# Two gate projections as seven products of quarters at the head of a layer, and the first products of two MLP groups side by side, in a two-layer hybrid encoder

## The chip, the cores and the metric

The kernel runs on one core of a Trainium2 chip. The metric is device time in microseconds of one execution of the whole program, which is both layers. Three runs of the kernel before gave 2899.88, 2901.86 and 2904.1 us; the median is 2901.86 us.

## What is computed

640 tokens (512 of one prompt, and 8 groups of 16) of width 1024 go through two layers in fp32. A layer is an RMS norm, one wide projection that feeds three mixers, a merge by gates, an output projection, and an MLP:

```
u = rms_norm(x, norm1_g);  z = u @ w_in
(xa, ga, mq, mk, mv, mo, mi, mf, aq, ak, av, g_a, g_b, g_c) = split(z)
y_a = (rg_lru(conv(xa)) * gelu(ga)) @ w_oa            # branch a
y_b = (rms_norm(mlstm(mq, mk, mv, ...)) * sigmoid(mo)) @ w_ob   # branch b
y_c = banded_sink_attention(rope(aq), rope(ak), av) @ w_oc      # branch c
mix = sigmoid(g_a + b0) * y_a + sigmoid(g_b + b1) * y_b + sigmoid(g_c + b2) * y_c
x = x + mix @ w_out
x = x + square(relu(rms_norm(x, norm2_g) @ w_up)) @ w_down
```

The three gate projections g_a, g_b and g_c are 1024 by 1024 each. The scale of the norm depends on the token alone, so the kernel multiplies it in after a projection.

## The kernel before

Every fp32 product is made of three products of a rounded high part and a low rest (hi·hi, hi·lo, lo·hi). A weight job loads 1 MB from DRAM into `wraw`, and each quarter of it is split by ScalarE (line 164, `whi`) and VectorE (line 166, `wlo`). `jobs` is the list of the weight jobs in the order in which the program takes them (lines 325 to 351); `next_w` prepares one job ahead.

`gemm_w` makes 256 output channels: two accumulators `acc` (there are two such buffers) of 48 matmuls of 320 columns each, 96 per job. A gate of one branch is four such jobs. `strassen_w` makes 256 channels of `w_up` with seven products of half-sized blocks in place of eight, 84 matmuls of 320 columns; VectorE adds the blocks of weights (`wsum`) and ScalarE and VectorE split the sums too. In before it serves the MLP alone.

A layer of before runs in this order: norm; the recurrent branch (LRU), whose projections run in turn with its scans; two jobs of gate b; attention (`attention`, with a third and a fourth job of gate b, and `branch_a(0)`, in it); `branch_a(1)` to `branch_a(3)`, each of which is a job of gate a and a job of `w_oa`; the mLSTM, head after head; four jobs of gate c, `gate(2)`; the merge; the output projection; the MLP. What the text writes is not what the engines run: a scheduler sorts the instructions by simulated times and priorities, and each engine then runs its own list in order. A job that comes later in the text is so drawn forward into places where an earlier stage waits, as far as its operands and its buffers allow.

Attention takes the heads in eight pairs (`prompt_pair`). For a pair, TensorE makes the scores (L847), VectorE takes the maxima (L822, L823), ScalarE the exponentials (L825, L826), VectorE the quotient (L827 to L830), TensorE transposes (L869), ScalarE and VectorE copy the result out (L871), and TensorE multiplies by the values (L877). Two groups of decode tokens (`sample_group`, L901 to L937) follow the fourth and the eighth pair. In the mLSTM a head's prompt chunks pass a state from one to the next (L672 to L690), and its decode tokens load, update and store eight state blocks (`sample`: L577 the keys' round trip over DRAM, L585 the load of a block `cb`, L589 and L590 its split, L593 and L597 the products, L599 the update, L601 the store).

The norm (`norm_scale`, L378 to L394) sums squares by matmuls with `ones` (L383), computes `rtok` in a chain of small VectorE instructions (L120 to L125), and spreads it over the partitions (L392 to L394) as `rbc`. Every evacuation of a projection multiplies by `rbc`.

Of the kernel before, what the change touches and what calls it, by code (L numbers as in the profile page):

```python
# [75 lines left out]
def trunk(ctx: ExitStack, tc: tile.TileContext, I, O):  # L76
# [92 lines left out]
    def prep(j, *hfs):  # L169
        ap, n, kind = jobs[j]  # L170
        out = ready.setdefault(j, [])
        if kind == "d":
# [6 lines left out]
            return  # L179
        if kind == "s":  # L180
# [9 lines left out]
            out.append(parts(a11, 128))  # L190
            s1 = add(a21, a22, ALU.add)
            yield
            out.append(parts(s1, 128))
# [12 lines left out]
            out.append(parts(s3, 128))  # L206
            out.append(last)
            yield
            return
# [22 lines left out]
    def next_w():  # L232
        j = cur[0]
        cur[0] += 1
        finish(j)
        if jobs[j][2] == "w":
            finish(j + 1)
        else:
            step()
        return ready.pop(j)  # L240

    def strassen_w(xs, epi):

        w = next_w()
# [4 lines left out]
        def product(nm):  # L249
            ws = w[("p1", "p5", "p2", "p3", "p6", "p7", "p4").index(nm)]  # L250
            first = nm in ("p1", "p5", "p2")
# [65 lines left out]
    for l in range(depth):  # L317
        win = I["w_in"][l]

        def cols(c, n=256):  # L320
            return (win[:, c:c + n], n)
# [4 lines left out]
        gc = [cols(C_G[2] + 256 * j) for j in range(4)]  # L326
        oa, ob, oc, ow = [[(I[nm][l][:, 256 * j:256 * j + 256], 256) for j in range(4)] for nm in ("w_oa", "w_ob", "w_oc", "w_out")]
        for k, j in LRU_ORDER:
            jobs.append(cols((C_XA, C_GA)[k] + 256 * j))
        jobs += [gb[0], gb[1], cols(C_AKV), gb[2]]  # L330
        for j in range(4):
            if j == 3:
                jobs += [ga[0], oa[0]]
            jobs.append(cols(C_AQ - 8, 264) if j == 0 else cols(C_AQ + 256 * j))
            if j == 1:
                jobs.append(gb[3])
        for j in range(1, 4):
            jobs += [ga[j], oa[j]]
        for j in range(4):
            jobs += seq[j]  # L340
        jobs += gc + oc + ob
        jobs += [ow[0], ow[2], ow[1], ow[3]]
        for kind, i in MLP_ORDER[l == depth - 1]:
            if kind == "s":
                jobs.append((I["w_up"][l][:, 256 * i:256 * i + 256], 256, "s"))
# [63 lines left out]
    cv, cvh = vectors(0)  # L409
    xpool = tc.tile_pool(name="xp0", bufs=8)  # L410
    xp = xpool.__enter__()
    with tc.tile_pool(name="ld", bufs=1) as ld:
# [19 lines left out]
        for m in range(8):  # L432
# [16 lines left out]
        dve.tensor_tensor(vv[:, 0:5], xss[:, 0:5], xss[:, 5:10], ALU.add)  # L449


# [287 lines left out]
    def attention(l, ap):  # L739
# [206 lines left out]
        for j in range(4):  # L946
# [11 lines left out]
            if j == 3:  # L958
                branch_a(0)
# [24 lines left out]
    for l in range(depth):  # L984
# [17 lines left out]
        norm_scale(vv[:, 0:5] if l == 0 else None)  # L1002
        xpool.__exit__(None, None, None)
        if l > 0:
            hdpool.__exit__(None, None, None)

        ngate = [0, 0, 0]
        kept = []

        def gate(i, keep=False):  # L1010
            def evac(m, acc):
# [4 lines left out]
                act.activation(sg, sg, AF.Tanh, bias=half(V_BG + i, k), scale=0.5)  # L1016
                if keep:
                    kept.append(sg)
                else:
                    act.dma_start(gdr[i][128 * k:128 * k + 128, :], sg)  # L1020
            gemm_w(u, evac)

        def branch_a(j):

            gate(0, True)

            def evac(m, acc):
                sg = kept.pop(0)
                dve.scalar_tensor_tensor(halves(sg), halves(sg), 1.0, acc[:, :, 0:320], op0=ALU.add, op1=ALU.mult)
                k = 2 * j + m  # L1030
                sp.dma_start(mdr[128 * k:128 * k + 128, :], sg)
            gemm_w(hg, evac)
# [174 lines left out]
        gate(1)  # L1207
        gate(1)
        with tc.tile_pool(name="at", bufs=1, reuse_waits="tile") as ap:
# [8 lines left out]
        gtp = gtpool.__enter__()  # L1218
        for j in range(1, 4):
            branch_a(j)  # L1220
            if j == 1:
                mlstm_gates(l, gp, gtp)
        hgpool.__exit__(None, None, None)
# [16 lines left out]
        xpool = tc.tile_pool(name=f"xp{l + 1}", bufs=8, reuse_waits="tile")  # L1240
        xp = xpool.__enter__() if l < depth - 1 else ctx.enter_context(xpool)
# [75 lines left out]
        dve.tensor_tensor(tt[:, 0:5], rtok[:, 0:5], rtok[:, 0:5], ALU.mult)  # L1317

# [12 lines left out]
        def up(i):  # L1331
# [36 lines left out]

            product = strassen_w(operand, epi)
            before = pend[0]  # L1370
# [19 lines left out]

        for n, (kind, i) in enumerate(MLP_ORDER[last]):
            if kind == "s":
# [72 lines left out]
```

## Time and profile before

| quantity | value |
|---|---|
| median of three runs | 2901.86 us |
| the profiled execution | 2899.9 us |
| its span in the trace | 2898.1 us |
| mean granted TensorE clock | 0.995 of full speed |
| TensorE matmul busy | 2839.4 us, 98% |
| VectorE busy | 1853.8 us, 64% |
| ScalarE busy | 1312.4 us, 45% |

PE is TensorE's matmul row, PEld its weight loads, DVE is VectorE, ACT is ScalarE, SP the engine that issues most DMAs. Matmuls overlap in their pipeline, so their busy time is longer than the time from one issue to the next. A granted clock of 1.00 is 2.4 GHz, and 0.5 is 1.2 GHz.

### The profile page before, as it was taken

Reading aid. Unit: us, or ns where it says so; the run is one execution under the profiler, and the core shown is the slowest. Engines: PE = TensorE matmul, PEld = TensorE weight load, DVE = VectorE, ACT = ScalarE, POOL = GpSimd, SP = SyncE. Lnnn points to the kernel's source line nnn. Section 1 sums busy time; section 2 is a strip of 40 time slices with the busy share of each in tenths; the row PEclk is TensorE's granted clock in tenths of the full one; section 3 lists DMA queues with packets and bytes.
Section 4 is the critical chain, followed back from the end, with each engine's and each line's share of the span. In section 5 each row is a group of like instructions: output and inputs, shape, how many; then the busy total and the mean of one; then the engine's idle time right before and its main releaser. Section 6 shows DMA issues by size and latency. Waiting matters only on the chain. (4 is left out here: it accounts for less than half of the span.)

```text
span 2898.1 us, 50789 instructions
## 1 busy us (share of the span) xinstructions
PE 2839.4 (98%) x20134; PEld 2799.9 (97%) x20134; DVE 1853.8 (64%) x3758; ACT 1312.4 (45%) x2767; POOL 26.7 (1%) x65
## 2 busy tenths in 40 slices
PE   8999999999999999999999999999999999999999
PEld 8999999999999999999999999999999999999999
DVE  7967566444565677676679676655445646667772
ACT  5764444333442445444357544443444324443452
POOL 0000000000000000000000000000000000000000
PEclk9999999999999999999999999999999999999999
DMA  5242224444573322222322322334445733222222
GB/s 174 65 123 81 76 82 123 120 136 138 158 259 125 104 72 81 81 80 81 113 67 79 116 73 84 96 101 147 131 141 152 264 110 102 74 88 73 80 81 81
DMA packets 276878, 319.53 MB, mean 110 GB/s; under 512 B 26424, under 2 KB 231016, under 8 KB 276608
## 3 DMA queue, kind: packets, MB, share of 16 engines
q1 hardware_dynamic: 267104, 300.03, 33.8%
q10 hardware_dynamic: 9536, 16.26, 1.6%
q8 instruction: 158, 2.59, 0.4%
q14 instruction: 80, 0.66, 0.1%
HBM read 255.76 MB, written 62.04 MB: 110 GB/s over the span
## 5 line engine op out<-in xcount | busy, mean ns | idle before, releaser
L293 PE MATMUL acc<-at,whi 128*128 128x320 f32 x5120 | 818.0, 312 | 6.9 <-ACT at L133 2.8
L293 PEld LDWEIGHTS acc<-at,whi 128*128 128x128 f32 x5120 | 765.3, 189 | 10.2 <-ACT at L133 3.4
L164 ACT CAST whi<-wraw 128x512 fp32r<-128x512 f32 x680 | 406.9, 619 | 512.7 <-PE acc L293 186.9
L166 DVE TENSOR_TENSOR wlo<-wraw,whi 128x512 fp32r<-128x512 f32 x680 | 451.3, 693 | 173.7 <-ACT whi L164 113.5
L311 PE MATMUL acc<-whi,at 128*128 128x256 f32 (+1 forms) x3040 | 408.5, 284 | 16.9 <-DVE qT L626 4.5
L293 PE MATMUL acc<-at,wlo 128*128 128x320 f32 x2560 | 415.6, 310 | 0.0
L311 PEld LDWEIGHTS acc<-whi,at 128*128 128x128 f32 x3040 | 378.2, 188 | 22.1 <-DVE qT L626 5.5
L293 PEld LDWEIGHTS acc<-at,wlo 128*128 128x128 f32 x2560 | 384.1, 188 | 0.7
L255 PE MATMUL acc<-at,whi 128*128 128x320 f32 x1536 | 266.9, 314 | 8.4 <-ACT at L130 5.5
L255 PEld LDWEIGHTS acc<-at,whi 128*128 128x128 f32 x1536 | 236.9, 191 | 14.4 <-ACT at L130 6.1
L311 PE MATMUL acc<-wlo,at 128*128 128x256 f32 (+1 forms) x1520 | 218.6, 282 | 0.2 <-DVE wlo L166 0.2
L311 PEld LDWEIGHTS acc<-wlo,at 128*128 128x128 f32 x1520 | 196.4, 188 | 0.6 <-DVE wlo L166 0.5
L277 PE MATMUL psb<-at,whi 128*128 128x320 f32 x896 | 171.1, 309 | 0.0
L277 PE MATMUL acc<-at,whi 128*128 128x320 f32 x896 | 169.0, 309 | 0.0
L255 PE MATMUL acc<-at,wlo 128*128 128x320 f32 x768 | 143.8, 310 | 0.0
L277 PEld LDWEIGHTS psb<-at,whi 128*128 128x128 f32 x896 | 141.6, 188 | 0.0
L277 PEld LDWEIGHTS acc<-at,whi 128*128 128x128 f32 x896 | 140.9, 188 | 0.0
L164 ACT CAST whi<-wsum 128x512 fp32r<-128x512 f32 x128 | 79.0, 619 | 129.1 <-PE acc L277 93.3
L255 PEld LDWEIGHTS acc<-at,wlo 128*128 128x128 f32 x768 | 121.5, 190 | 0.0
L166 DVE TENSOR_TENSOR wlo<-wsum,whi 128x512 fp32r<-128x512 f32 x128 | 87.8, 689 | 46.9 <-ACT whi L164 45.1
L277 PE MATMUL acc<-at,wlo 128*128 128x320 f32 x448 | 101.8, 308 | 0.0
L277 PE MATMUL psb<-at,wlo 128*128 128x320 f32 x448 | 100.6, 308 | 0.0
(372 smaller groups left out, 3613.1 us busy)
## 6 DMA issues: line engine op xcount, KB each, us to landing
wraw<-in_w_in SPq DMA_DIRECT2D x160, 512.0 KB
wraw<-in_w_up SPq DMA_DIRECT2D x64, 512.0 KB
wraw<-in_w_down SPq DMA_DIRECT2D x64, 512.0 KB
cb<-in_state_mlstm_C SPq DMA_DIRECT2D x64, 256.0 KB
out_C_s<-cb SPq DMA_DIRECT2D x64, 256.0 KB
gdr<-sg ACTq DMA_DIRECT2D x32, 320.0 KB
rl<-ydr SPq DMA_DIRECT2D x32, 320.0 KB
sg<-gdr SPq DMA_DIRECT2D x32, 320.0 KB
```

The source lines that it names most:

```text
L164: act.copy(hi if shape else hi[:, :, :src.shape[-1]], src)
L166: dve.tensor_tensor(lo if shape else lo[:, :, :src.shape[-1]], src, h.bitcast(F32), ALU.subtract)
L255: pe.matmul(bank[nm], ws[i][:, k, :], xs(nm, k)[:, part], start=(first and i == 0 and k == 0 and part == 0), stop=(i == 1 and k == 3), ski ...
L277: pe.matmul(o[s], lhs, hs[k][:, part, 320 * s:320 * s + 320], start=(k == 0 and i == 0 and part == 0), stop=(i == 1 and k == 3))
L293: pe.matmul(acc[:, s, 0:320], lhs, xs[k][:, part, 320 * s:320 * s + 320], start=(i == 0 and k == 0 and part == 0), stop=(i == 1 and k == 7),)
L311: pe.matmul(o, xs[k][:, part, 128 * t:128 * t + 128], wt[:, k % KQ, 0:n], start=(i == 0 and k == 0 and part == 0), stop=(i == 1 and k == 7),)
```

## The change

Gates a and c are computed first in a layer, right after two jobs of gate b, by `strassen_gates`: eight jobs through `strassen_w`, with 84 matmuls in place of 96. Before that, VectorE and ScalarE form the sums of the activations that the seven products need (`t12`, `t34`: four pairs of tiles). The gates are written to DRAM (`gdr`), and gate a is read back by `branch_a`, which is now a job of `w_oa` alone. `branch_a(1)` stands where `branch_a(0)` stood, `branch_a(0)` moves one step ahead; a job of gate b stands at the end of the LRU and one in attention. No gate is left between `branch_a` and the mLSTM's end, and after the mLSTM the attention's output is reloaded with no job between.

In the MLP, the groups 0 and 1 of `w_up` begin side by side: their first products are issued in turn, and `norm_scale` stands behind them. For that the first two operands of group 1 are loaded early and its raw weights are loaded a second time (job kinds `e` and `r`).

```diff
+    out += [("e", 1), ("s", 0), ("r", 1)]
     for i in range(15):
-        out.append(("s", i))
+        if i > 1:
+            out.append(("s", i))
...
+        jobs += [gb[0], gb[1]]
+        jobs += [(a, n, "s") for a, n in ga + gc]
         for k, j in LRU_ORDER:
             jobs.append(cols((C_XA, C_GA)[k] + 256 * j))
-        jobs += [gb[0], gb[1], cols(C_AKV), gb[2]]
+        jobs += [gb[2], cols(C_AKV), gb[3]]
         for j in range(4):
             if j == 3:
-                jobs += [ga[0], oa[0]]
+                jobs.append(oa[1])
             jobs.append(cols(C_AQ - 8, 264) if j == 0 else cols(C_AQ + 256 * j))
             if j == 1:
-                jobs.append(gb[3])
-        for j in range(1, 4):
-            jobs += [ga[j], oa[j]]
+                jobs.append(oa[0])
+        jobs += oa[2:]
         for j in range(4):
             jobs += seq[j]
-        jobs += gc + oc + ob
+        jobs += oc + ob
...
+    def strassen_gates(l, ut, u, xs, vec, half):
+        t12, t34, xg = [], [], {}
+        for i in range(4):
+            for k in (i, 4 + i):
+                xg[k] = ut.tile([128, NT], F32, name="xg", tag="xg", bufs=2)
+                act.activation(xg[k], xs[k], AF.Copy, scale=vec(V_N1, k))
+            a, b = xg[i], xg[4 + i]
+            t = ut.tile([128, NT], F32, name="ut12", tag="ut12", bufs=1)
+            dve.tensor_tensor(t[:, 0:320], a[:, 320:640], a[:, 0:320], ALU.subtract)
+            dve.tensor_tensor(t[:, 320:640], b[:, 320:640], t[:, 0:320], ALU.subtract)
+            t12.append(act_tile(ut))
+            split(t12[i], t)
...
+            return strassen_w(operand, epi)
...
+        with tc.tile_pool(name="ut", bufs=8, reuse_waits="tile") as ut:
+            sums[0] = ut
+            gate(1)
+            gate(1)
+            strassen_gates(l, ut, u, xs, vec, half)
...
         def branch_a(j):
-            gate(0, True)
-
             def evac(m, acc):
-                sg = kept.pop(0)
+                k = 2 * j + m
+                sg = tr.tile([128, NT], F32, name="sg", tag="sg")
+                with tc.issue_after(wlast[0].ins):
+                    sp.dma_start(sg, gdr[0][128 * k:128 * k + 128, :])
...
         gate(1)
-        gate(1)
         with tc.tile_pool(name="at", bufs=1, reuse_waits="tile") as ap:
             attention(l, ap)
...
-        for j, n in enumerate((4, 0, 3, 0)):
-            yc += reload(ydr[1], hdp, range(len(yc), len(yc) + n))
-            gate(2)
-        yc += reload(ydr[1], hdp, range(7, 8))
+        yc += reload(ydr[1], hdp)
...
-        norm_scale()
-
-        dve.tensor_tensor(rbc, rbc, rbc, ALU.mult)
...
+        early, early_run = {1: next_w()}, (0, 1)
+        p_0 = up(0)
+        p_0("p1")
+        p_0("p5")
+        p_1 = up(1)
+        p_1("p1")
+        p_1("p5")
...
+        norm_scale()
```

TensorE, the seventh pair of attention's eight, in the kernel before (L847 the scores, L869 the transposes, L293 matmuls of `gemm_w`):

```order
L847 MATMUL psb<-kh_2338,qp_2361 128x64 x2
L847 MATMUL psb<-kh_2338,qp_2361 128x128 x2
L847 MATMUL psb<-kh_2338,qp_2361 128x192 x12
L293 MATMUL acc<-at,whi 128x320 x23
L293 MATMUL acc<-at,wlo 128x320 x16
L293 MATMUL acc<-at,whi 128x320 x4
L869 MATMUL psb<-cs,prob_2368 128x128 x2
L293 MATMUL acc<-at,whi 128x320 x2
L869 MATMUL psb<-cs,prob_2369 128x128 x4
L293 MATMUL acc<-at,whi 128x320 x6
L869 MATMUL psb<-cs,prob_2370 128x128 x4
L869 MATMUL psb<-cs,prob_2371 128x128 x4
```

The same place in the changed kernel (L930 scores, L952 transposes, L960 products with the values, L1052 and L1054 the next queries' transposes):

```order
L930 MATMUL psb<-kh_3684,qp_3707 128x64 x2
L930 MATMUL psb<-kh_3684,qp_3707 128x128 x2
L930 MATMUL psb<-kh_3684,qp_3707 128x192 x12
L952 MATMUL psb<-cs,prob_3714 128x128 x2
L952 MATMUL psb<-cs,prob_3715 128x128 x4
L960 MATMUL psb<-pT,vd 128x256
L952 MATMUL psb<-cs,prob_3716 128x128 x4
L952 MATMUL psb<-cs,prob_3717 128x128 x4
L960 MATMUL psb<-pT,vd 128x256 x2
L1052 MATMUL psb<-cs,q 128x128 x4
L960 MATMUL psb<-pT,vd 128x256 x4
L1054 MATMUL psb<-cs,q 128x128
```

In this place 51 of `gemm_w`'s matmuls stand between the scores and the last transposes of before, and none in the changed kernel; the three other pairs of attention's second half read the same there, in both layers. The jobs that stood here are gates, which are now at the layer's head, and jobs of `w_oa`, which the changed order has used up ahead of the fifth pair; what follows next, the mLSTM's first job, needs a buffer that attention holds.

TensorE in the mLSTM's last head, before (L679, L682, L686, L672 the chunks' products; L293 here is gate c):

```order
L293 MATMUL acc<-at,wlo 128x320 x2
L679 MATMUL psb<-vt,pt 128x257
L686 MATMUL psb<-vt,kw 128x257 x2
L672 MATMUL psb<-qT,kT 128x128 x2
L293 MATMUL acc<-at,wlo 128x320 x14
L293 MATMUL acc<-at,whi 128x320 x10
L679 MATMUL psb<-vt,pt 128x257
L682 MATMUL psb<-cp,qs 128x257 x2
L686 MATMUL psb<-vt,kw 128x257 x2
L672 MATMUL psb<-qT,kT 128x128 x2
L293 MATMUL acc<-at,whi 128x320 x22
```

The changed kernel there (L762, L765, L769, L755 the same products, L676 the first of the decode state's):

```order
L762 MATMUL psb<-vt,pt 128x257
L765 MATMUL psb<-cp,qs 128x257 x2
L769 MATMUL psb<-vt,kw 128x257 x2
L755 MATMUL psb<-qT,kT 128x128 x2
L303 MATMUL acc<-at,whi 128x320 x8
L762 MATMUL psb<-vt,pt 128x257
L676 MATMUL psb<-ch,qm 128x258
```

The matmuls of gate c have left the gaps between the chunks' products. What is left between them is part of one `w_oc` job, drawn forward.

VectorE at the start of the second layer, before, from the norm's sum on (`sm` and `lwl` belong to the LRU):

```order
L385 TENSOR_SCALAR vv<-psb 128x5
L120 TENSOR_SCALAR rtok<-vv 128x5
L121 TENSOR_SCALAR rtok<-rtok 128x5
L123 TENSOR_TENSOR tt<-rtok 128x5
L124 SCALAR_TENSOR_TENSOR tt<-tt,vv 128x5
L1070 TENSOR_SCALAR sm<-sm 128x8
L125 SCALAR_TENSOR_TENSOR rtok<-tt,rtok 128x5
L1071 RECIPROCAL sm<-sm 128x8
L123 TENSOR_TENSOR tt<-rtok 128x5
L1072 TENSOR_TENSOR sm<-sm 128x8
L124 SCALAR_TENSOR_TENSOR tt<-tt,vv 128x5
```

The changed kernel there (`ut`, `xg` and `at` are the activations' sums of `strassen_gates` and their split, `wsum` the sums of weights):

```order
L396 TENSOR_SCALAR vv<-psb 128x5
L471 TENSOR_TENSOR ut_16717<-xg 128x320
L476 TENSOR_TENSOR ut_16723<-xg 128x320
L122 TENSOR_SCALAR rtok<-vv 128x5
L472 TENSOR_TENSOR ut_16717<-xg,ut_16717 128x320
L188 TENSOR_TENSOR wsum<-wraw 128x512
L123 TENSOR_SCALAR rtok<-rtok 128x5
L477 TENSOR_TENSOR ut_16723<-xg,ut_16717 128x320
L188 TENSOR_TENSOR wsum<-wsum,wraw 128x512
L125 TENSOR_TENSOR tt<-rtok 128x5
L133 TENSOR_TENSOR at<-ut_16717,at 128x640
L168 TENSOR_TENSOR wlo<-wsum,whi 128x512
```

The chain from `vv` to `rtok` now has large instructions between its small ones: up to the end of the chain 8 subtractions of 320 columns, 4 splits of 640 columns and 5 instructions on weights of 512 columns.

## Rows read from the trace of the kernel before

**Rows 1.** The page's span and busy time of each engine.

```profile
span 2898.1 us, 50789 instructions
PE 2839.4 (98%) x20134; PEld 2799.9 (97%) x20134; DVE 1853.8 (64%) x3758; ACT 1312.4 (45%) x2767; POOL 26.7 (1%) x65
```

**Rows 2.** Stretches: us, busy of PE, PEld, DVE, ACT, POOL; clock, DMA share, GB/s.

```profile
900.00:950.00 50.00, 50.00 (x342) 50.00 (x342) 24.38 (x33) 13.22 (x21) 0.00 (x0) 1.00 0.34 107
1050.00:1100.00 50.00, 50.00 (x344) 50.00 (x343) 35.46 (x60) 21.69 (x38) 0.00 (x0) 1.00 0.25 75
316.00:475.00 159.00, 156.55 (x1137) 153.34 (x1137) 103.30 (x233) 69.50 (x202) 7.62 (x12) 1.00 0.29 90
786.00:832.00 46.00, 46.00 (x321) 45.67 (x320) 32.72 (x81) 18.09 (x41) 0.00 (x0) 1.00 0.70 220
1010.00:1030.00 20.00, 15.51 (x82) 14.60 (x81) 15.10 (x37) 7.93 (x13) 0.00 (x0) 0.74 0.12 31
2450.00:2470.00 20.00, 15.52 (x81) 14.61 (x80) 14.95 (x37) 8.05 (x14) 0.00 (x0) 0.74 0.10 30
```

**Rows 3.** TensorE in time, the seventh pair: start, duration, what, count.

```profile
416.69 1.93 PE L847 MATMUL psb<-kh,qp 128*128 128x64 f32 x16
426.63 1.04 PE L869 MATMUL psb<-cs,prob 128*128 128x128 f32 x8
429.27 1.02 PE L877 MATMUL psb<-pT,vd 128*128 128x256 f32 x4
430.13 0.60 PE L969 MATMUL psb<-cs,q 128*128 128x128 f32 x4
436.80 1.93 PE L847 MATMUL psb<-kh,qp 128*128 128x64 f32 x16
```

**Rows 4.** TensorE by line, 416.69 to 436.80 us: xcount, busy us, mean ns.

```profile
L293 PE MATMUL acc<-at,whi 128*128 128x320 f32 x60 | 11.4, 323 | 0.0
L293 PE MATMUL acc<-at,wlo 128*128 128x320 f32 x32 | 5.0, 308 | 0.0
```

**Rows 5.** VectorE in time, the same pair; in brackets idle time and its end.

```profile
423.28 1.03 DVE L830 TENSOR_TENSOR prob<-prob,ssm 128x384 f32<-128x384 f32 x2
428.58 0.69 DVE L871 COPY pT<-psb 128x512 f32<-128x512 f32 x1 [1.95 <-PE psb L877]
```

**Rows 6.** ScalarE in time, the same pair.

```profile
419.30 0.31 ACT L825 ACTIVATE prob<-psb,ssm 128x64 f32<-128x64 f32 x1 [4.38 <-DVE ssm L823]
```

**Rows 7.** TensorE by line, 786 to 832 us: xcount, busy us, mean ns.

```profile
L293 PE MATMUL acc<-at,whi 128*128 128x320 f32 x160 | 25.7, 309 | 0.0
L293 PE MATMUL acc<-at,wlo 128*128 128x320 f32 x92 | 15.8, 309 | 0.0
```

**Rows 8.** VectorE, mLSTM's last head: where its decode part begins and ends.

```profile
786.55 0.35 DVE L677 TENSOR_SCALAR kw<-ktok,tokq 128x256 f32<-128x256 f32 x1
821.70 0.42 DVE L698 TENSOR_TENSOR num<-csum,psb 128x256 f32<-128x256 f32 x1
```

**Rows 9.** VectorE and TensorE in time, the start of the second layer.

```profile
1464.18 0.17 DVE L385 TENSOR_SCALAR vv<-psb 128x5 f32<-128x5 f32 x1 [3.71 <-PE psb L383]
1468.72 0.69 DVE L166 TENSOR_TENSOR wlo<-wraw,whi 128x512 fp32r<-128x512 f32 x1
1469.40 0.16 DVE L125 SCALAR_TENSOR_TENSOR rtok<-tt,rtok 128x5 f32<-128x5 f32 x1
1472.12 0.48 DVE L1104 TENSOR_TENSOR xq<-acc,rbc 128x320 f32<-128x320 f32 x1
1469.61 1.38 PE L392 MATMUL psb<-cs,rtok 128*128 128x128 f32 x10 [1.70 <-DVE rtok L125]
1473.22 3.00 PE L293 MATMUL acc<-at,whi 128*128 128x320 f32 x10 [1.61 <-DVE xq L1106]
```

**Rows 10.** TensorE in time, the start of the first layer's MLP.

```profile
1016.24 0.63 PE L255 MATMUL acc<-at,whi 128*128 128x320 f32 x1 [2.80 <-ACT at L130]
```

More of the change, by code (lines that the diff above doesn't have):

```diff
@@ L189, in prep @@
             yield
-            out.append(parts(a11, 128))
+            if kind != "r":
+                out.append(parts(a11, 128))
             s1 = add(a21, a22, ALU.add)
             yield
-            out.append(parts(s1, 128))
+            if kind != "r":
+                out.append(parts(s1, 128))
+            if kind == "e":
+                return
             s2 = add(s1, a11, ALU.subtract)
@@ L237, in next_w @@
             finish(j + 1)
+            if j + 1 < len(jobs) and jobs[j + 1][2] == "e":
+                finish(j + 2)
         else:
@@ L240, in next_w, with strassen_w @@
         return ready.pop(j)
-    def strassen_w(xs, epi):
-        w = next_w()
+    def strassen_w(xs, epi, early=None):
+        w = early if early is not None else next_w()
         acc, b3 = ps_acc(), ps_small()
@@ L249, in product @@
         def product(nm):
+            if early is not None and nm == "p2":
+                w.extend(next_w())
             ws = w[("p1", "p5", "p2", "p3", "p6", "p7", "p4").index(nm)]
@@ L409, in trunk @@
     cv, cvh = vectors(0)
-    xpool = tc.tile_pool(name="xp0", bufs=8)
+    xpool = tc.tile_pool(name="xp0", bufs=8, side="right")
     xp = xpool.__enter__()
@@ L449, in trunk, with operand, job, copy @@
         dve.tensor_tensor(vv[:, 0:5], xss[:, 0:5], xss[:, 5:10], ALU.add)
+    def strassen_gates(l, ut, u, xs, vec, half):
[10 more added lines that the diff above has]
+            split(t12[i], t)
+            t_ = ut.tile([128, NT], F32, name="ut34", tag="ut34", bufs=1)
+            dve.tensor_tensor(t_[:, 0:320], b[:, 320:640], a[:, 320:640], ALU.subtract)
+            dve.tensor_tensor(t_[:, 320:640], b[:, 0:320], t[:, 320:640], ALU.subtract)
+            t34.append(act_tile(ut))
+            split(t34[i], t_)
+        def operand(nm, i):
+            t, c = {"p1": (u[i], 0), "p2": (u[4 + i], 0), "p3": (u[4 + i], 1),
+                    "p5": (t12[i], 0), "p6": (t12[i], 1), "p7": (t34[i], 0), "p4": (t34[i], 1)}[nm]
+            return t[:, :, 320 * c:320 * c + 320]
+        def job(i, j):
+            sg, kept = {}, {}
+            def copy(nm, src):
+                t = ut.tile([128, 320], F32, name=nm, tag=nm, bufs=2 if nm == "g5" else 1)
+                act.copy(t, src)
+                return t
+            def done(c):
+                k = 2 * j + c
+                act.activation(sg[c], sg[c], AF.Tanh, bias=half(V_BG + i, k), scale=0.5)
+                act.dma_start(gdr[i][128 * k:128 * k + 128, :], sg[c])
+            def epi(nm, b):
+                if nm == "p1":
+                    kept["p1"] = copy("g1", b["p1"])
+                elif nm == "p5":
+                    kept["p5"] = copy("g5", b["p5"])
+                elif nm == "p2":
+                    sg[0] = tr.tile([128, NT], F32, name="sg", tag="sg")
+                    dve.tensor_tensor(sg[0][:, 0:320], kept["p1"], b["p2"], ALU.add)
+                elif nm == "p6":
+                    u2 = copy("g2", b["p6"])
+                    dve.tensor_tensor(sg[0][:, 320:640], u2, b["p3"], ALU.add)
+                    dve.tensor_tensor(sg[0], sg[0], rbc, ALU.mult)
+                    done(0)
+                elif nm == "p7":
+                    sg[1] = tr.tile([128, NT], F32, name="sg", tag="sg")
+                    dve.tensor_tensor(sg[1][:, 320:640], kept["p5"], b["p7"], ALU.add)
+                    dve.tensor_tensor(sg[1][:, 320:640], sg[1][:, 320:640], rbc[:, 320:640], ALU.mult)
+                elif nm == "p4":
+                    dve.tensor_tensor(sg[1][:, 0:320], b["p4"], rbc[:, 0:320], ALU.mult)
+                    done(1)
+            return strassen_w(operand, epi)
+        before = None
+        for i, j in [(0, j) for j in range(4)] + [(2, j) for j in range(4)]:
+            product = job(i, j)
+            for nm in ("p1", "p5", "q7", "p2", "p3", "q4", "p6"):
+                if nm[0] == "p":
+                    product(nm)
+                elif before is not None:
+                    before("p" + nm[1])
+            before = product
+        before("p7")
+        before("p4")
@@ L958, in attention @@
             if j == 3:
-                branch_a(0)
+                branch_a(1)
             gemm_x(u, ev_q, 264 if j == 0 else 256)
             if j == 1:
-                gate(1)
+                branch_a(0)
             qv = q.rearrange("p t (h d) -> p t h d", d=64)
@@ L1007, in trunk, with gate @@
         ngate = [0, 0, 0]
-        kept = []
-        def gate(i, keep=False):
+        def gate(i):
             def evac(m, acc):
@@ L1218, in trunk @@
         gtp = gtpool.__enter__()
[L1219 to L1222, printed above, removed]
+        branch_a(2)
+        mlstm_gates(l, gp, gtp)
+        branch_a(3)
         hgpool.__exit__(None, None, None)
@@ L1232, in trunk @@
         yc = []
-        for j, n in enumerate((4, 0, 3, 0)):
-            yc += reload(ydr[1], hdp, range(len(yc), len(yc) + n))
-            gate(2)
-        yc += reload(ydr[1], hdp, range(7, 8))
+        yc += reload(ydr[1], hdp)
         mix = []
-        xpool = tc.tile_pool(name=f"xp{l + 1}", bufs=8, reuse_waits="tile")
+        xpool = tc.tile_pool(name=f"xp{l + 1}", bufs=8, reuse_waits="tile", side="right")
         xp = xpool.__enter__() if l < depth - 1 else ctx.enter_context(xpool)
@@ L1367, in epi, with run @@
                     unit(1)
-            product = strassen_w(operand, epi)
+            product = strassen_w(operand, epi, early.pop(i, None))
+            if i in early_run:
+                return product
+            run(product)
+            return None
+        def run(product):
             before = pend[0]
@@ L1389, in down @@
             gemm_d([hid[4 * g + i] for i in range(4)], evac)
-        for n, (kind, i) in enumerate(MLP_ORDER[last]):
+        early, early_run = {1: next_w()}, (0, 1)
[5 more added lines that the diff above has]
+        p_1("p5")
+        for nm in ("p2", "p3", "p6"):
+            p_0(nm)
+        p_1("p2")
+        p_0("p7")
+        p_1("p3")
+        p_0("p4")
+        p_1("p6")
+        pend[0] = p_1
+        norm_scale()
+        dve.tensor_tensor(rbc, rbc, rbc, ALU.mult)
+        dve.tensor_tensor(tt[:, 0:5], rtok[:, 0:5], rtok[:, 0:5], ALU.mult)
+        for n, (kind, i) in enumerate(MLP_ORDER[last][3:]):
             if kind == "s":
```

16 lines of the change are left out of this document (5 added, 11 removed).

## The prediction

> **What bounds the kernel now.** I read the page's busy times first, then the stretches, then TensorE in time. TensorE's matmul row is busy for 98% of the span, VectorE for 64% [rows 1]. Busy matmuls overlap, so I take the price of one from a stretch that is full at clock 1.00: 342 matmuls in 50 us, 0.146 us each [rows 2]. The reader is to see in the other stretches of [rows 2] how even the two stages with long chains are full. From 316 to 475 us, attention's second half, TensorE is busy for 156.55 of 159 us; from 786 to 832 us, the mLSTM's last head, for all 46. In both, the chain of the stage does not fill TensorE; matmuls of `gemm_w` do, which the order has drawn into its gaps: 92 of them inside one pair of heads [rows 4], 252 in the last head [rows 7]. Only the MLP's start is poor: 82 matmuls in 20 us at a mean clock of 0.74, and 81 in the second layer [rows 2].
>
> So the kernel is bound by the number of matmuls as long as each gap has a filler. The change removes matmuls, and it takes the fillers away.
>
> **Matmuls removed: -28 us.** Gates a and c are 8 jobs in a layer, 16 in all. Each goes from 96 matmuls to 84, so 192 go, at 0.146 us: 28.1 us. VectorE has more to do in such a job (sums and splits of weights). The MLP, with the same seven products, shows TensorE full at 344 matmuls in 50 us with VectorE busy for 35.46 [rows 2], so I price that at nothing; without this cover it would be the excess over 12.3 us a job. Extra DMAs (gate a out and back, 1 MB of `w_up` twice) find the DMA engines at a share of 0.25 to 0.34 there: nothing.
>
> **MLP start: -10 us.** At 0.146 us, 82 matmuls are 12.0 us of the 20, so 8.0 are lost in the first layer, and 8.2 in the second. A wait of 2.80 us for the last operand is among them [rows 10], the rest are shorter waits and matmuls at a lower clock. With two groups side by side there are matmuls on the operands that are ready, but the last operand comes no sooner. I take 5 us back of 8 in each layer; the ends are 0 and 16 for both together.
>
> **Attention, pairs five to eight: +50 us.** The order shows no foreign matmul here any more. What remains is the chain of one pair after the other. From the first score to the end of the last quotient it is 416.69 to 424.31 us, 7.6 us [rows 3, 5]; ScalarE's exponentials stand in it and wait for VectorE's maxima [rows 6]. Behind it come eight transposes, 1.0 us, a copy, 0.7, and the products of the pair's second half. In the trace four of those take 0.86 us up to the next instruction [rows 3], and there are eight: about 1.9 with the end. That is 11.2 us a pair. TensorE's own work in a pair is the 20.1 us between two pairs' scores [rows 3] less 92 x 0.146 = 13.4: 6.7 us. So it idles 4.5 us a pair, 18 for four. The fifth pair shares VectorE with the last queries' norm: I add 4 us, an estimate, since VectorE's large instructions there delay its maxima. The decode group, two such chains behind each other, I put at one pair's loss, 5 us. 27 in all, less the 2.45 us that TensorE idles in this stretch already: 25 us a layer. Ends: 12, if the chain shrinks to 10 us since weights' splits no longer cut into it and the estimates fall away; 50, if the work left in it, some 34 us, also runs at a lower clock for most of the time.
>
> **mLSTM, last head: +30 us.** Four jobs of gate c filled it. Of its 46 us, 252 x 0.146 = 36.8 were theirs, and 9.2 its own. In the changed order 24 matmuls of `w_oc` stand here, 3.5 us: 12.7 us of work. The decode chain took 35.1 us, from 786.55 to 821.70 [rows 8], with fillers in between. A part of it was waiting behind these fillers, a part was loads, splits and stores in turn. I take 28 us without them, nearer to the row than to the work, so a loss of 15 us a layer. Ends: 5 (chain of 18) and 22 (chain as before).
>
> **Start of a layer: +18 us.** VectorE's chain from `vv` to `rtok` ran in 5.4 us in the second layer [rows 9]. Into it the change puts 8 subtractions of 320 columns at 0.48 [rows 9], 4 splits of 640 at about twice a subtraction less the fixed part (0.8, an estimate), and 5 instructions on weights at 0.69: 10.5 us. Some 13 small steps of about 0.2 us remain between them, so `rtok` comes about 13 us after `vv`. All matmuls that can go ahead of it stand ahead of the norm's sum in the order, both accumulators are full, and only `rbc` frees them. TensorE idles about 15 us where it had waited 1.70 and 1.61 [rows 9]: +12. In the first layer 72 matmuls, 10.5 us, run beside the chain, which is as long: +6, an estimate with ends of 2 and 12. For both layers the ends are 10 and 27.
>
> One gate job instead of two stands between the recurrent branch and attention. I count nothing: 96 matmuls, 14 us, still cover that step; without them it could cost up to the 14 us of the other job.
>
> **Sum.** -28 - 10 + 50 + 30 + 18 = +60 us, on the profiled execution's 2899.9 us: 2960 us. That execution lies 2 us below the median of the three runs, so I leave it at 2960.
>
> **A rule against my clock.** I have priced the gaps with the clock at 2.4 GHz. In the trace the wait of 2.80 us stands in a stretch whose mean clock is 0.74, a mix of 2.4 and 1.2 GHz, while the stretch 316 to 475 with its 2.45 us of scattered idle time kept 1.00 [rows 2, 10]. The Trainium skill (TensorE: Matmul & The Clock Gate, "Why this matters for your kernels") says to keep bursts of matmuls free of idle gaps, or the clock falls back to half. By that rule each new gap of four us would bring slow matmuls behind it. The rows agree for the one gap and do not show a series of them; the result of the rule is the second rival below.
>
> **Rivals.** First, faster: the chains pack, since without a job's splits on ScalarE and VectorE a pair needs hardly more than TensorE's 6.7 us, and a head hardly more than its 12.7. Then both stages cost about 4 us a layer together, and the sum is -28 - 10 + 18 + 8 = -12: 2888 us. It decides from the point where attention and the mLSTM together lose less than 10 us a layer. For it speaks that TensorE was 98% busy and that VectorE spent much of a pair on other work; against it, that the 7.6 us up to the last quotient hold maxima, exponentials and quotients that wait for each other on three engines [rows 3, 5, 6]. The skill's rule to improve the most contended engine first (Perfetto Trace Analysis, "Identifying the Most-Contended Engine") points this way; its next section, "Optimization Strategy", points the other way: stages with different limits gain from being interleaved. The full stretches of [rows 2] bear out the second.
>
> Second, slower still: the gaps bring the clock down. Attention's 34 us of work a layer would gain up to 25 us of it back as loss, the mLSTM's 13 us up to 8, and the start a few: about +60 for both layers together when half of it hides in waits that are there anyway, 3020 us. For it speaks the MLP's start, against it that the gaps are shorter than that one in part.
>
> Third, one stage of the two keeps some filler on the chip or loses only its lower end: 2920 to 2935 us.
>
> **Chances.** The forecast, 2935 to 2985 us, 0.45; the second rival 0.22; the third, with less loss in one or both stages, 0.18; the first 0.15, in whose band faster is 0.11 and no change 0.04. About 0.2% (6 us) is what a measurement here can tell from no change. So faster 0.11, same 0.05, slower 0.84. The range, 2905 to 3025 us, leaves out most of the first rival and the far end of the second.
>
> **What would show it.** Right: in the changed profile, TensorE's waits in attention's second half are for `pT`, `prob` or `qp`, at 3 to 6 us a pair, and scores of two pairs start about 11 us apart; in the last head it waits for `ch` and `cb`, about 15 us in all; at the second layer's start one wait of 12 to 15 us ends with `rbc`; the count of matmuls in the order is lower by 192; the MLP's start loses about 3 us. Wrong: pairs 7 us apart, a last head of under 18 us, or a start without a long wait; or a clock of 0.5 over whole stretches, which would be the second rival.

## The result, and the profile after

The changed kernel takes 3064.83 us (median of four runs, 3061.76 to 3066.28), against 2901.68 us before. The ratio is 1.0558, with a 95% interval of 1.0546 to 1.0571. The forecast was 2960 us with a range of 2905 to 3025, so the direction held and the size did not: +163 us in place of +60.

The page of the changed kernel, its span, the engines' busy time and the clock in 40 slices:

```profile
span 3064.4 us, 50998 instructions
PE 2871.3 (94%) x19942; PEld 2810.6 (92%) x19942; DVE 1978.4 (65%) x3984; ACT 1379.9 (45%) x2895; POOL 26.8 (1%) x65
PEclk9999998899989999999989999989999899999999
```

Three numbers divide the loss. TensorE runs 192 matmuls fewer than in [rows 1], at 0.146 us: -28 us. It is idle for 3064.4 - 2871.3 = 193.1 us, where it had been idle for 2898.1 - 2839.4 = 58.7: +134 us. The span grew by 166 us, so 166 + 28 - 134 = 60 us are left by difference: the same matmuls took longer, at a lower clock (a mean of 0.966 over the span, 0.995 before). The forecast had -28, +88 for the stages, and nothing for a clock that falls behind the new gaps.

Stretches of the changed kernel, columns as in [rows 2]: five of attention's second half (the pairs five to eight, the decode group), the mLSTM's last head, the LRU's end and the second layer's start:

```profile
500.00:515.00 15.00, 7.42 (x32) 6.46 (x33) 11.93 (x24) 5.45 (x22) 0.95 (x1) 0.66 0.10 22
515.50:529.70 14.20, 9.23 (x49) 7.98 (x49) 8.88 (x24) 6.25 (x25) 0.00 (x0) 0.76 0.06 21
529.70:544.00 14.30, 9.03 (x50) 7.67 (x49) 9.29 (x25) 6.50 (x25) 0.00 (x0) 0.76 0.05 18
544.00:558.50 14.50, 10.07 (x59) 8.96 (x60) 8.44 (x24) 6.32 (x24) 0.43 (x1) 0.76 0.05 18
558.50:575.00 16.50, 10.74 (x64) 9.51 (x63) 8.90 (x20) 5.54 (x23) 5.22 (x10) 0.79 0.05 17
864.00:932.00 68.00, 46.29 (x245) 40.23 (x246) 42.34 (x103) 25.59 (x60) 0.00 (x0) 0.80 0.54 171
296.00:318.00 22.00, 10.76 (x60) 10.07 (x59) 14.90 (x27) 11.01 (x20) 3.29 (x5) 0.70 0.39 124
1525.00:1565.00 40.00, 22.98 (x128) 22.37 (x129) 34.39 (x69) 26.21 (x41) 0.00 (x0) 0.73 0.25 78
```

In the first five TensorE idles 28 us, and its clock is 0.66 to 0.79, where the whole of attention's second half had run at 1.00 [rows 2]. The last head idles 21.7 us at 0.80, where it had been full. The LRU's end, for which I had counted nothing, idles 11.2 us at 0.70. The start of the second layer idles 17.0 us at 0.73.

What TensorE waited for in the changed kernel (us in total, times, longest):

```profile
PE psb L952 <- DVE prob L913: 34.4, 8, 7.7
PE acc L321 <- ACT vd L863: 17.3, 2, 8.7
PE psb L804 <- DVE num L798: 15.7, 5, 6.6
PE psb L403 <- DVE rtok L127: 12.9, 2, 11.9
PE psb L676 <- ACT ch L672: 12.0, 9, 2.5
PE psb L930 <- DVE qp L1059: 10.7, 8, 1.7
```

Each of these waits stands at one of the four places, and none at the seven products themselves. TensorE in time over one pair of heads, the answer to [rows 3]:

```profile
517.19 2.00 PE L930 MATMUL psb<-kh,qp 128*128 128x64 f32 x16 [1.72 <-DVE qp L1059]
522.47 1.55 PE L952 MATMUL psb<-cs,prob 128*128 128x128 f32 x6 [3.27 <-DVE prob L913]
529.48 0.27 PE L1054 MATMUL psb<-cs,q 128*128 128x128 f32 x1
531.47 2.01 PE L930 MATMUL psb<-kh,qp 128*128 128x64 f32 x16 [1.72 <-DVE qp L1059]
536.75 1.55 PE L952 MATMUL psb<-cs,prob 128*128 128x128 f32 x6 [3.27 <-DVE prob L913]
```

A pair takes 14.28 us, with two waits, 1.72 and 3.27 us: 5.0 together, where I had put 4.5. What the forecast lacks are 14.28 - 5.0 - 6.7 = 2.6 us, by which TensorE's own work in a pair got longer. Stretches of 1 us in the same pair show why; the last columns are the clock, the DMA share and GB/s:

```profile
532.00:533.00 1.00, 1.00 (x11) 1.00 (x11) 0.81 (x3) 0.00 (x0) 0.00 (x0) 1.00 0.04 14
533.00:534.00 1.00, 0.48 (x5) 0.30 (x3) 0.97 (x4) 0.01 (x1) 0.00 (x0) 0.67 0.00 0
534.00:535.00 1.00, 0.00 (x0) 0.00 (x0) 0.59 (x2) 1.00 (x6) 0.00 (x0) 0.50 0.00 0
...
539.00:540.00 1.00, 1.00 (x6) 1.00 (x5) 0.59 (x1) 0.00 (x0) 0.00 (x0) 0.50 0.00 0
540.00:541.00 1.00, 1.00 (x8) 0.95 (x7) 0.31 (x1) 0.58 (x1) 0.00 (x0) 0.92 0.00 0
541.00:542.00 1.00, 1.00 (x9) 0.87 (x8) 0.80 (x2) 0.08 (x1) 0.00 (x0) 1.00 0.00 0
```

The clock falls to 1.2 GHz between 533 and 534 us, as the scores end (by the mean of 0.67 at about 533.3, just before the second wait begins at 533.5), and comes back to 2.4 GHz after 540 us, when the transposes have been running for three. So each pair does its transposes and first products at half clock, and in the next pair the clock falls again.

At the LRU's end TensorE waits for an instruction that has nothing to do with the LRU. TensorE there, and then ScalarE:

```profile
313.96 3.78 PE L321 MATMUL acc<-whi,at 128*128 128x256 f32 x16 [8.66 <-ACT vd L863]
```

```profile
312.55 0.74 ACT L135 ACTIVATE at<-hgt 128x640 fp32r<-128x640 f32 x1 [1.82 <-DVE hgt L1266]
313.45 0.46 ACT L863 ACTIVATE vd<-acc,rtok 128x256 f32<-128x256 f32 x1
```

The evacuation `vd`, which frees an accumulator, stands on ScalarE behind the LRU's last outputs (L135), and these wait for VectorE.

In the last head, VectorE's decode part from its first to its last row, the same two instructions as in [rows 8], and the two stretches in it and behind it:

```profile
881.27 0.35 DVE L760 TENSOR_SCALAR kw<-ktok,tokq 128x256 f32<-128x256 f32 x1
910.12 0.42 DVE L781 TENSOR_TENSOR num<-csum,psb 128x256 f32<-128x256 f32 x1
```

```profile
881.27:910.54 29.27, 19.04 (x88) 15.36 (x88) 20.45 (x46) 13.56 (x31) 0.00 (x0) 0.74 0.69 218
910.54:932.00 21.46, 11.75 (x61) 10.61 (x62) 14.09 (x39) 4.89 (x10) 0.00 (x0) 0.74 0.55 180
```

The decode part takes 28.9 us by the rows that read 35.1 before. TensorE idles 10.2 us in it and another 9.7 us behind it, where it waits for the head's scaled rows (`num`, L798) and then for an accumulator.

### The profile page after: what moved, and what is told of

It is laid out like the page before. It is cut to its first block, busy times and chain, and to the rows that moved or that the text cites. A ratio compares the mean times of both kernels' runs of the same rounds, so it can differ in the third digit from the quotient of the medians.

```text
span 3064.4 us, 50998 instructions
## 1 busy us (share of the span) xinstructions
PE 2871.3 (94%) x19942; PEld 2810.6 (92%) x19942; DVE 1978.4 (65%) x3984; ACT 1379.9 (45%) x2895; POOL 26.8 (1%) x65
## 4 chain that ended last, share of the span: by engine, by line
PE 80%; DVE 8%; DMA 5%; ACT 4%; issue 2%; SPq 0%; POOL 0%; ACTq 0%; DVEq 0%; POOLq 0%
PE acc L303 24%; PE acc L265 16%; PE acc L321 15%; PE acc L287 6%; PE psb L287 6%; PE psb L265 3%; DMA out_C_s<-cb 2%; PE psb L960 2%; PE psb L952 1%; DMA rl<-ydr 1%; DVE wlo L168 1%; DMA cb<-in_state_mlstm_C 1%; PE psb L1233 1%; PE psb L769 1%; PE psb L930 1%
## 5 line engine op out<-in xcount | busy, mean ns | idle before, releaser
L303 PE MATMUL acc<-at,whi 128*128 128x320 f32 x4096 | 655.4, 314 | 19.6 <-DVE sg L1140 9.7
L166 ACT CAST whi<-wraw 128x512 fp32r<-128x512 f32 (+1 forms) x664 | 398.0, 620 | 567.9 <-PE acc L303 210.1
L303 PEld LDWEIGHTS acc<-at,whi 128*128 128x128 f32 x4096 | 618.5, 191 | 23.0 <-issue 15.3
L168 DVE TENSOR_TENSOR wlo<-wraw,whi 128x512 fp32r<-128x512 f32 (+1 forms) x664 | 439.5, 686 | 201.9 <-ACT whi L166 148.5
L321 PE MATMUL acc<-whi,at 128*128 128x256 f32 (+1 forms) x3040 | 416.7, 287 | 34.6 <-ACT vd L863 17.3
L265 PE MATMUL acc<-at,whi 128*128 128x320 f32 x2304 | 393.7, 312 | 11.5 <-ACT s L1419 5.4
L265 PEld LDWEIGHTS acc<-at,whi 128*128 128x128 f32 x2304 | 350.9, 189 | 19.9 <-ACT s L1419 9.1
L303 PE MATMUL acc<-at,wlo 128*128 128x320 f32 x2048 | 327.1, 309 | 0.0
L303 PEld LDWEIGHTS acc<-at,wlo 128*128 128x128 f32 x2048 | 307.2, 188 | 0.0
L265 PE MATMUL acc<-at,wlo 128*128 128x320 f32 x1152 | 216.5, 310 | 0.2 <-DVE wlo L168 0.2
L166 ACT CAST whi<-wsum 128x512 fp32r<-128x512 f32 x192 | 118.9, 620 | 187.3 <-PE acc L287 90.6
L265 PEld LDWEIGHTS acc<-at,wlo 128*128 128x128 f32 x1152 | 182.2, 189 | 0.5 <-DVE wlo L168 0.4
L168 DVE TENSOR_TENSOR wlo<-wsum,whi 128x512 fp32r<-128x512 f32 x192 | 131.6, 687 | 58.9 <-ACT whi L166 57.8
L287 PE MATMUL acc<-at,whi 128*128 128x320 f32 x896 | 169.1, 309 | 0.1
L287 PEld LDWEIGHTS acc<-at,whi 128*128 128x128 f32 x896 | 140.7, 188 | 0.4 <-ACT whi L166 0.4
L287 PE MATMUL acc<-at,wlo 128*128 128x320 f32 x448 | 101.8, 308 | 0.0
```

The lines of the kernel that those rows point to most:

```text
L166: act.copy(hi if shape else hi[:, :, :src.shape[-1]], src)
L168: dve.tensor_tensor(lo if shape else lo[:, :, :src.shape[-1]], src, h.bitcast(F32), ALU.subtract)
L265: pe.matmul(bank[nm], ws[i][:, k, :], xs(nm, k)[:, part], start=(first and i == 0 and k == 0 and part == 0), stop=(i == 1 and k == 3), ski ...
L287: pe.matmul(o[s], lhs, hs[k][:, part, 320 * s:320 * s + 320], start=(k == 0 and i == 0 and part == 0), stop=(i == 1 and k == 3))
L303: pe.matmul(acc[:, s, 0:320], lhs, xs[k][:, part, 320 * s:320 * s + 320], start=(i == 0 and k == 0 and part == 0), stop=(i == 1 and k == 7),)
L321: pe.matmul(o, xs[k][:, part, 128 * t:128 * t + 128], wt[:, k % KQ, 0:n], start=(i == 0 and k == 0 and part == 0), stop=(i == 1 and k == 7),)
```

## The experiments

The theory: the matmuls are as fast as ever, and the loss is that of cover. The gates were what filled the chains' gaps, and each gap costs its idle time and matmuls at half clock. A first rival holds that the seven products cost, by their sums, splits and copies. A second holds that the forecast's sizes stand and the rest lies elsewhere.

**Ordinary jobs in the same place.** The gates stay at the head, by 96 matmuls a job.

```diff
-        jobs += [(a, n, "s") for a, n in ga + gc]
+        jobs += ga + gc
...
-            strassen_gates(l, ut, u, xs, vec, half)
+            for i in (0, 0, 0, 0, 2, 2, 2, 2):
+                gate(i)
```

> The changed kernel with gates a and c in the same place, but by ordinary jobs of 96 matmuls. If the loss is one of cover (the gates have left the gaps of attention and of the mLSTM), all waits stay and 192 matmuls come back at 0.146 us: 3064.8 + 28 = 3093 us. If the seven products themselves are what costs (sums, splits and copies on VectorE and ScalarE), this kernel is faster than the changed one, below 3050 us.

Measured: 3077.07 us, ratio to before 1.0602 (1.0586 to 1.0617). That is 12 us over the changed kernel, not 28, and not below it. So the products do not carry the loss: with ordinary ones nearly all of it stays. Of the 28 us, 16 are missing because without the sums VectorE's chain at the start is short; the wait for `rtok` is 2.8 us where the changed kernel had 12.9 in two. The fifth run tests that by itself.

```profile
PE psb L952 <- DVE prob L913: 34.4, 9, 7.7
PE acc L321 <- ACT vd L863: 17.3, 2, 8.7
PE psb L403 <- DVE rtok L127: 2.8, 1, 2.8
```

**Gate c back behind the mLSTM.** Four `gate(2)` jobs with the reloads between them, as before; gate a stays at the head.

```diff
...
-        yc += reload(ydr[1], hdp)
+        for j, n in enumerate((4, 0, 3, 0)):
+            yc += reload(ydr[1], hdp, range(len(yc), len(yc) + n))
+            gate(2)
+        yc += reload(ydr[1], hdp, range(7, 8))
```

> The changed kernel with gate c again by four ordinary jobs behind the mLSTM, gate a still by seven products at the head. Theory of cover: the last head's gaps are filled again (about 36 us a layer, of it part clock), 96 matmuls come back (+14 us): 3064.8 - 72 + 14 = 3007 us, with TensorE full in the last head and attention's waits as in the changed kernel. If attention alone bears the loss: 3079 us. By my forecast's size for this head (15 us a layer): 3049 us.

Measured: 3015.99 us, 1.0387 (1.0369 to 1.0404). With the 14 us of the 96 matmuls that came back, the last heads and what follows them gave back 3064.8 - 3016.0 + 14 = 63 us, 31 a layer, twice the forecast's 15. The stretch is full again at 1.00, and of the next 25 us TensorE is busy for 24.19:

```profile
815.00:860.00 45.00, 45.00 (x306) 43.96 (x305) 20.27 (x49) 17.72 (x39) 0.00 (x0) 1.00 0.39 115
```

**Gate a back as filler in attention.** A job of gate a ahead of each job of `w_oa`; gate c stays at the head.

```diff
-                jobs.append(oa[1])
+                jobs += [ga[1], oa[1]]
...
+            gemm_w(u, evac_g)
...
             def evac(m, acc):
...
-                sg = tr.tile([128, NT], F32, name="sg", tag="sg")
-                with tc.issue_after(wlast[0].ins):
-                    sp.dma_start(sg, gdr[0][128 * k:128 * k + 128, :])
+                sg = kept.pop(0)
```

> The changed kernel with gate a again by ordinary jobs, each ahead of its job of w_oa, gate c still by seven products at the head. Theory of cover: attention's second half is full again (about 50 us a layer), 96 matmuls come back (+14 us): 3064.8 - 100 + 14 = 2979 us, last head as in the changed kernel. By my forecast's size (25 us a layer): 3029 us. If the low clock comes from elsewhere than from these gaps, pairs of heads still show 0.5 of full clock.

Measured: 3018.52 us, 1.0397 (1.0382 to 1.0413). It gives back 46 + 14 = 60 us, against 50 by the forecast and 100 by the theory as I had put it. The two stretches show where the rest is:

```profile
450.00:525.00 75.00, 74.46 (x527) 72.77 (x525) 52.47 (x116) 30.72 (x95) 0.95 (x1) 1.00 0.33 102
525.00:550.00 25.00, 18.18 (x105) 15.42 (x105) 12.26 (x34) 11.06 (x45) 5.64 (x10) 0.86 0.03 11
```

The pairs are full at 1.00 until the four jobs are used up. By the order of the jobs one is still missing in this attention, the one that the change has moved to the head, and the last pair and the decode group pay for it at 0.86.

**The MLP as before.** Norm ahead of the groups, no early operands; gates as changed.

```diff
-    out += [("e", 1), ("s", 0), ("r", 1)]
...
         for j in range(4):
             gemm_w(mix, ev_out)
+        norm_scale()
...
```

> The changed kernel with the MLP's order, jobs and norm as before; gates as changed. By the forecast's term for the MLP's start (5 us gained a layer) it is 10 us slower than the changed kernel, 3075 us. If the two groups side by side gain nothing (the trace shows 38 us from 1087 to 1125 at a clock of 0.91), it is within 3 us of 3065.

Measured: 3058.52 us, 1.0536 (1.052 to 1.0551), 6 us faster than the changed kernel. The forecast had the term at -10. The last run tests its sign by itself.

**The sums behind the chain.** Everything as changed, but the instructions that form `t12` and `t34` are ordered behind `rtok`.

```diff
-        dve.tensor_scalar(rt16[:, 0:5], rtok[:, 0:5], 1.0 / 16.0, None, op0=ALU.mult)
+        nlast[0] = dve.tensor_scalar(rt16[:, 0:5], rtok[:, 0:5], 1.0 / 16.0, None, op0=ALU.mult)
...
+            with tc.issue_after(nlast[0].ins):
+                dve.tensor_tensor(t[:, 0:320], a[:, 320:640], a[:, 0:320], ALU.subtract)
...
```

> The changed kernel with the sums of activations (t12, t34) ordered behind the chain to rtok. If those instructions on VectorE are what delays rbc, the wait of 12 us before the second layer's rtok falls to 2 to 4 us, and the start gives back what the run with ordinary jobs kept there, about 16 us: 3049 us. If TensorE would wait for the sums themselves instead, it stays at 3060 to 3065 us.

Measured: 3049.72 us, 1.0507 (1.0491 to 1.0523): 15 us back, as expected. TensorE's wait there, in this kernel:

```profile
PE psb L404 <- DVE rtok L127: 1.6, 1, 1.6
```

**Useless matmuls in the waits.** Scores computed again, never read, in pairs five to eight.

```diff
+                if H == 1 and pair >= 4:
+                    wacc = ps_acc()
+                    for r in range(28):
+                        pe.matmul(wacc[:, r % 2, 0:192], q[:, r % 8].rearrange("p a d -> p (a d)"), kh[g][:, 0, 0:192],
+                                  start=True, stop=True)
```

> The changed kernel with 28 useless matmuls of 192 columns (scores computed again, never read) behind the scores of the second half of each of pairs five to eight, 224 in all, about 2.6 us a pair at full clock. If a pair's 14.3 us are waits alone, they fill part of the waits and nothing moves: 3065 us, or up to 20 us more where they get in the way. If the low clock is a good part of a pair (PE at 0.50 for 6 of the 14 us), they hold the clock up and pairs shorten to about 12 us: 8 x 2 = 16 us faster, 3049 us.

Measured: 3143.94 us, 1.0831 (1.0815 to 1.0848). Neither theory said 79 us more. The first half of attention lost its filler too. A likely cause, which no run isolates, is that the extra matmuls take an accumulator in the middle of attention, and that the jobs of `w_oa`, which come later in the text, now get theirs after it. The row is this kernel, with waits of up to 10.4 us for `q`:

```profile
400.00:500.00 100.00, 72.13 (x440) 66.31 (x439) 61.93 (x151) 41.08 (x149) 0.95 (x1) 0.78 0.10 34
```

The changed kernel in this stretch:

```profile
400.00:500.00 100.00, 99.73 (x749) 97.92 (x747) 63.04 (x147) 42.68 (x127) 0.95 (x1) 1.00 0.36 117
```

It does not tell idle time from clock, for which it was meant. That division rests on the traces alone.

**Another filler in the last head.** The matmuls are those of the changed kernel. Branch c's merge takes its input from other buffers and writes its rows to DRAM, so that its four jobs can be drawn forward.

```diff
-        yc += reload(ydr[1], hdp)
+        yc = reload(ydr[1])
...
+        def sink_c(k, sg):
+            mx = tr.tile([128, NT], F32, name="mx", tag="sg")
...
+            sp.dma_start(cdr[128 * k:128 * k + 128, :], mx)
```

> The changed kernel with branch c's merge made free to be drawn into the mLSTM's last head: attention's output is reloaded into the buffers of u, and the merged rows go over DRAM (8 stores and 8 loads of 320 KB a layer more). The matmuls are the same ones. Theory of cover: any filler will do, the last head's loss goes, 60 to 65 us for both layers: 3000 to 3005 us. If it was gate c's own place that mattered, or the extra DMAs collide with the decode state's, above 3040 us.

Measured: 3037.47 us, 1.0468 (1.0450 to 1.0485): 27 us back, where 60 to 65 were expected. The head itself is nearly full, and the next stage is late:

```profile
864.00:932.00 68.00, 65.03 (x439) 62.83 (x438) 44.99 (x107) 25.40 (x59) 0.00 (x0) 1.00 0.70 218
932.00:962.00 30.00, 23.01 (x134) 22.03 (x133) 14.04 (x21) 9.44 (x16) 0.00 (x0) 0.83 0.78 247
```

```profile
949.65 2.30 PE L304 MATMUL acc<-at,whi 128*128 128x320 f32 x8 [4.24 <-ACT at L133]
954.69 7.52 PE L304 MATMUL acc<-at,whi 128*128 128x320 f32 x32 [2.75 <-ACT at L133]
```

These waits are for the mLSTM's own output, which goes over DRAM and is split again; `w_oc`'s jobs had covered that trip when they stood behind the mLSTM. Any matmul fills the gap, but one that is taken from another gap opens that one.

**Put together.** Three jobs of gate c by seven products behind one job of gate b, sums late, two jobs of gate b at the LRU's end, the rest as filler, the merge as above, the MLP as before: 72 matmuls fewer than before.

```diff
+        jobs += [gb[0]]
+        jobs += [(a, n, "s") for a, n in gc[:3]]
...
+        jobs += [gb[1], gb[2], cols(C_AKV), gb[3]]
+            if j == 2:
+                jobs += gc[3:]
```

> Put together from what the runs showed: three of gate c's four jobs by seven products at the head behind one job of gate b, sums behind rtok, two jobs of gate b at the LRU's end, gate a and gate c's fourth job as fillers in attention, branch c's merge as filler in the mLSTM, MLP as before. 72 matmuls less than before in all, 10.5 us. Theory of cover: the gaps are full again, and it is 2902 - 10 + 0 to 8 for the sums at the two starts: 2892 to 2900 us. If the seven products at the head need more than the sums (a wait of their own), it is over 2905 us.

Measured: 2945.83 us, 1.0149 (1.0131 to 1.0167), the best of the kernels with gates by seven products, and slower than before. It misses the expected 2892 to 2900 us by 46, on the side of "a wait of their own". Attention is full in it (39.87 of 40 us from 495 to 535), and the two longest sums of waits lie for the most part where cover went to attention and the last head. Of the first, 5.1 and 4.4 us lie at the two layers' starts, where TensorE waits for the activations' sums, and the rest at the MLP's starts; of the second, 7.4 and 6.9 us lie where the mLSTM's output is read back:

```profile
PE acc L265 <- ACT at L131: 15.0, 7, 2.8
PE acc L303 <- ACT at L131: 14.9, 8, 4.2
```

**Two jobs at the LRU's end.** As changed, with one ordinary job of gate b moved there from the head.

```diff
-        jobs += [gb[0], gb[1]]
+        jobs += [gb[0]]
...
-        jobs += [gb[2], cols(C_AKV), gb[3]]
+        jobs += [gb[1], gb[2], cols(C_AKV), gb[3]]
```

> The changed kernel with one of the two ordinary jobs of gate b moved from the layer's head to the LRU's end, so that two stand there again, as before. If one job was too short a cover there (TensorE waits 8.7 us for vd at 305 us, at a clock of 0.70 over 22 us), the wait goes and gives back about 10 us a layer, 20 in all, less what the head loses with one job fewer (0 to 15 us a layer): 3045 to 3065 us. If the job is worth the same in either place, 3065 us, and the wait only changes its place. If the LRU's end doesn't need it, the wait stays.

Measured: 3032.36 us, 1.0458 (1.0444 to 1.0473): 32 us faster than the changed kernel, more than the 20 expected. No wait for `vd` is left among TensorE's waits, and at the head the waits for `rtok` went from 12.9 to 14.7 us in total. Nearly all of the 32 us lies at the LRU's end. The projection of keys and values there, 120 matmuls, in the changed kernel and in this one:

```profile
294.69:324.53 29.84, 18.59 (x125) 17.91 (x124) 16.68 (x30) 15.46 (x30) 3.29 (x5) 0.77 0.30 94
298.59:312.76 14.17, 14.17 (x122) 14.17 (x121) 6.54 (x16) 6.04 (x14) 2.31 (x4) 1.00 0.60 188
```

That is 15.7 us in this layer, of which 11.2 were idle time and the rest a lower clock; the expected 10 had the idle time alone.

**The MLP's edit alone, on the kernel before.**

```diff
+        early, early_run = {1: next_w()}, (0, 1)
+        p_0 = up(0)
+        p_0("p1")
+        p_0("p5")
+        p_1 = up(1)
...
```

> The kernel before with the MLP's edit alone: two groups' first products side by side, operands early, norm behind. By the forecast's term: 2902 - 10 = 2892 us. By the run without that edit, which was 6 us faster than the changed kernel: 2905 to 2909 us, with the waits for s, x, ha and at at the MLP's start in place of the one wait of 2.8 us.

Measured: 2904.21 us against 2900.13, ratio 1.0014 (1.0005 to 1.0023), 4 us slower. In 45 us around the first layer's MLP start it runs

```profile
1010.00:1055.00 45.00, 38.74 (x239) 36.40 (x238) 37.22 (x75) 29.22 (x52) 0.00 (x0) 0.92 0.22 71
```

and the kernel before

```profile
1005.00:1050.00 45.00, 40.51 (x252) 39.60 (x251) 35.43 (x71) 28.14 (x50) 0.00 (x0) 0.89 0.22 68
```

13 matmuls fewer in the same time, 1.9 us a layer, although the clock is a little higher. The interval leaves out 1, so the term's sign was wrong.

## Why the prediction was wrong in size

**Attention, +50 forecast.** The chain was right and its idle time too: 27 us a layer in the forecast, 28 in the trace. The step that failed is "I have priced the gaps with the clock at 2.4 GHz". Of the 75 us from 500 to 575 TensorE works for 47, where the forecast put the work at some 34. In the pair shown above 2.6 us of the difference lie. I had the rule from the Trainium skill (TensorE: Matmul & The Clock Gate, "Why this matters for your kernels") beside a row that agreed, and gave it 0.22, because the gaps are shorter than the one at the MLP's start "in part". This trace shows that gaps of 1.72 and 3.27 us, one after the other, are enough. And "do not show a series of them" was a misreading of the rows: in [rows 9], behind waits of 1.70 and 1.61 us, ten matmuls take 3.00 us, 0.30 each where a full stretch has 0.146, and the trace has a clock of 0.50 there (1474 to 1476 us). The second rival's mechanism took place, and even its 3020 us were too few, since other terms were off as well.

**The LRU's end, nothing forecast.** "96 matmuls, 14 us, still cover that step" was wrong. TensorE waits 8.7 us in each layer for one accumulator, and moving one job there made the kernel 32 us faster, 15.7 us a layer at that place. I had looked for what the step needs, and not for what is queued ahead of its evacuation on ScalarE.

**The mLSTM's last head, +30 forecast.** 63 us came back with gate c. The chain was right: 28 us in the forecast, 28.9 in the trace, 35.1 before. What failed is "so a loss of 15 us a layer", which ended the loss with the decode part and priced the work in it at full clock. TensorE idles 10.2 us in that part at 0.74, and 9.7 us more behind it, for the head's scaled rows and for an accumulator, at 0.74 too. Gate c's matmuls had covered that end as well, and the forecast had no term for it. In all the trace has 21.7 us of idle time a layer, near the upper end of 22, and a clock of 0.80 on top.

**MLP start, -10 forecast.** It costs 4 to 6 us. The last operand comes no sooner, as the forecast said; the wait only moved, and I gave the rest a gain that no row supported.

**Start, +18 forecast.** With the sums behind `rtok` 15 us came back. In the second layer TensorE waits 11.9 us for `rtok` and 1.4 us behind it, where about 15 were forecast. This term held.

**Matmuls, -28 forecast.** All 192 are gone, and in the changed kernel no wait stands within the gates' seven products. Their gain is 28 us less what the sums cost at the start: the run with ordinary jobs is 12 us slower, and 12 + 15 or 16 is the 28.

**The first rival**, chains that pack into their gaps, did not show: a pair's waits are 5.0 us with ScalarE and VectorE free of other work, and from the first score to the last quotient it is 531.47 to 539.00 us, 7.5 where the forecast had 7.6.

What the single runs gave back can't be added up: a job that fills one gap comes from another. How much of the 60 us of slower matmuls lies in each stage was read from the clock in the traces, and no run separated it.

## What to carry to other kernels

In a kernel whose chains are covered by foreign matmuls, count the jobs that can cover and the gaps that need one, before a cheaper job is moved out of its gap. Here eight gate jobs a layer saved at most 28 us in number, and the change lost 191 elsewhere, some 20 of it by the sums at the start and the MLP's edit, the rest, as far as the runs show, where cover was gone. And price a gap with the clock that it brings: a stage that idles for a third of its time in short waits also does a good part of its work at 1.2 GHz.

## What the runs showed of the hardware

Waits of 1.72 and 3.27 us, with some 2 us of matmuls between them, kept TensorE's mean granted clock at 0.76 over whole pairs, while a stretch with 2.45 us of scattered idle time in 159 kept 1.00 [rows 2]. In the pair above the clock fell as the scores ended, shortly before the second wait, and it was back only after about 3 us of matmuls. In the run with useless matmuls, the second pair that has them has no second wait, and the clock fell all the same. TensorE there, and then the stretches:

```profile
486.65 2.36 PE L930 MATMUL psb<-kh,qp 128*128 128x64 f32 x16 [1.72 <-DVE qp L1064]
488.80 4.60 PE L946 MATMUL acc<-kh,qp 128*128 128x192 f32 x28
```

```profile
486.65:488.80 2.15, 2.15 (x16) 2.15 (x17) 1.43 (x4) 0.00 (x0) 0.00 (x0) 0.84 0.28 106
488.80:491.00 2.20, 2.20 (x12) 2.20 (x12) 1.05 (x5) 1.83 (x10) 0.00 (x0) 0.50 0.00 0
491.00:493.40 2.40, 2.40 (x20) 2.40 (x20) 1.78 (x7) 1.70 (x9) 0.00 (x0) 0.89 0.00 0
```

The clock was 1.00 during the wait of 1.72 us; it fell while the scores ran and came back while the useless matmuls ran, with TensorE busy throughout. A wait of 1.72 us does not always do this: in the kernel before, one stands ahead of 473.51 us, and the clock stayed at 1.00.
